# The last feed-forward product in two pieces: 388 tokens with features on the partitions, 128 tokens with tokens on the partitions

## The chip, the cores and the metric

The kernel runs on one core of one Trainium2 chip. The metric is the device time of one execution in microseconds; lower is better. The engines are named as in the profile: PE (TensorE), DVE (VectorE), ACT (ScalarE), POOL (GpSimd) and SP (SyncE, which only issues DMAs here).

## What is computed

One layer of a hybrid decoder for 1024 prompt positions and 8 sample rows, 1032 tokens of 1024 features. What matters here is the end of the layer: the feed-forward part and the second layer norm, over the features of each token.

```python
x1 = layer_norm(DN_ALPHA * x + mix, ln1_g, ln1_b)
ff = jnp.square(jax.nn.relu(x1 @ w_up + b_up)) @ w_down + b_down
ple = jax.nn.sigmoid(x1 @ w_ple_gate + b_ple_gate) * (p @ w_ple)
x2 = layer_norm(DN_ALPHA * x1 + ff + ple, ln2_g, ln2_b)
```

The output `o_y` has features on its rows (8 blocks of 128 features by 1032 tokens) and is put in order after the launch.

## The kernel before

Activations lie with features on the partitions: `acc[m]`, m = 0 to 7, is a block of 128 features by 1032 tokens, and holds the sum that the second layer norm takes. HF = 516 is half of the tokens, QT = 258 a quarter. Every f32 operand of a product is split into two parts of a shorter type, high and low (`split`, line 107: ACT copies the high part, DVE subtracts for the low one), and a product is three matmuls: high by high, high by low, low by high (`kmm`, line 1517).

The down projection is done by Strassen's scheme in seven products, in the order `DNO` (line 1425): P1, P2, P6, P7, P4, P5, P3. Each works on half of the tokens, half of the k range (16 slices of 128) and four blocks of 128 output features, `mp` = 0 to 3. The weights of a product are eight tiles of 128 by 1024: `dn_raw` (line 1450) loads a tile with one DMA on SP into one of three `raw` buffers, `split` turns it into high and low. For P3 the source is `sd["S4"]`, sums of weights that the kernel wrote to DRAM earlier. Four of the eight tiles of P3 go into the four rotating `hl` buffers, the last four (`n` = 52 to 55) into tiles named `dh`. Tile `2 * mp + c` holds the k slices 8c to 8c + 7 of block `mp`. The activations of a product are `hop[96 + k]`, k = 0 to 15, in SBUF.

The last product, P3, only adds to the second half of the tokens, blocks `acc[0]` to `acc[3]`. It is written out at the end of the kernel (the loops over `q` and `mp`): for each of the two quarters q = 2, 3 and each `mp`, 48 matmuls of 258 columns into a PSUM tile of `region2` (three in rotation), then a DVE add into `acc[mp]`. `sum_` keeps a running sum of the blocks in `sum2`.

The layer norm of feature-major tokens needs sums over partitions. They are f32 matmuls with a 128 by 128 matrix of equal values, `ones`, which leave the mean on every partition. `rsqrt_` (line 804) is an inverse root in nine dependent DVE operations. Quarter 2 is normalised by the generator `ln_steps` (line 1057), pulled while quarter 3 is multiplied. Quarter 3 is normalised by `ln_last` (line 1598) in steps: the mean of the first five finished blocks is subtracted early, squares are gathered as blocks finish, steps 7 and 8 put partial sums onto TensorE at k = 9 and 13 of the last block; step 9 does the rest: the last square, two reductions, the inverse root, and for each block a product with gain and inverse root on DVE, a scale and shift on ACT, and an output DMA (`ln2_out`, line 1514, on SP or ACT's queue). Its centering of six blocks is done by TensorE with `ident` and `nident` into PSUM.

The framework orders the instructions of each engine itself by readiness and program order; so operations of two parts that don't depend on each other mix on an engine. A value normaliser with tokens on the partitions exists elsewhere in the kernel (`v_norm`, line 840: `bn_stats`, `bn_aggr`, the same `rsqrt_` on a column for each token); so does a load in four DMAs with 512-byte pieces (`A_v`, line 184, for `w_v`).

## Time and profile before

| what | value |
|---|---|
| time, median of 3 runs | 1369.5 us (1369.17 to 1370.01) |
| time of the profiled execution | 1369.48 us |
| its span | 1367.7 us |
| TensorE busy | 1357.4 us, 99% |
| DVE busy | 907.6 us, 66% |
| ACT busy | 499.5 us, 37% |
| HBM over the span | 167 GB/s |

The span runs from the first to the last event of the core; the rest of the time lies around it. A busy time counts stretches in which an engine has at least one instruction in work. Matmuls are pipelined, so a matmul's duration is longer than the distance to the next one; the distance (pitch) is what counts for a sum. An f32 matmul stands as two records.

### The profile page before, as it was taken

To read this page: it belongs to the slowest core of one execution; us is meant where nothing else is said; L and a number is where in the kernel's file an instruction comes from. 1 tells how busy PE (TensorE), PEld (TensorE's weight loads), DVE (VectorE), ACT (ScalarE), POOL (GpSimd) and SP (SyncE) were. 2 spreads that over 40 slices of the span, in tenths; PEclk is the share of its full clock that TensorE was granted. 3 is DMA by queue.
4 is the path that set the end of the run, shared out by engine and by line. 5 is a ranking of instruction groups with operands and counts; after the bars stand their busy time and mean duration, and the time that the engine had idled before them with its cause. 6 is when DMAs were issued, how large, how long until landed. Compare 5 with 4: busy or idle time off the path is not lost.

```text
span 1367.7 us, 24910 instructions
## 1 busy us (share of the span) xinstructions
PE 1357.4 (99%) x10222; PEld 1336.6 (98%) x10222; DVE 907.6 (66%) x1590; ACT 499.5 (37%) x694; POOL 195.5 (14%) x318
## 2 busy tenths in 40 slices
PE   9999999999999999999999999999999999999997
PEld 8999999988999999999999999999999999999997
DVE  8929348346476656996787767755665575466957
ACT  3231231222241133554234444444454433244423
POOL 0320310125021112000003333201100000000000
PEclk9999999999999999999999999999999999999999
DMA  7573564532256667342346677645478764565421
GB/s 262 147 181 101 148 156 111 154 114 70 71 197 236 231 224 249 107 133 93 109 133 229 231 271 248 219 149 171 135 234 275 278 225 165 179 213 196 137 94 62
DMA packets 104418, 237.20 MB, mean 173 GB/s; under 512 B 11736, under 2 KB 40552, under 8 KB 104304
## 3 DMA queue, kind: packets, MB, share of 16 engines
q1 hardware_dynamic: 76800, 159.84, 37.1%
q0 software_dynamic: 22128, 72.09, 15.1%
q10 hardware_dynamic: 5376, 3.68, 1.1%
q8 instruction: 80, 1.31, 0.4%
q14 instruction: 34, 0.28, 0.1%
HBM read 160.72 MB, written 68.16 MB: 167 GB/s over the span
## 4 chain that ended last, share of the span: by engine, by line
PE 97%; DVE 1%; DMA 0%; issue 0%; ACT 0%; SPq 0%; ACTq 0%; DVEq 0%
PE q L1174 38%; PE q L1541 19%; PE big L146 8%; PE big L123 6%; PE big L124 6%; PE big L125 6%; PE q L1521 1%; PE q L1520 1%; PE q L1522 1%; PE vps L877 1%; PE vps L876 1%; PE vps L875 1%; PE sps L597 1%; PE kps L543 1%; PE gps L921 1%; PE yps L702 1%
## 5 line engine op out<-in xcount | busy, mean ns | idle before, releaser
L86 DVE TENSOR_TENSOR hl<-raw,hl 128x1024 fp32r<-128x1024 f32 (+1 forms) x174 | 210.3, 1210 | 158.3 <-ACT hl L109 157.1
L1541 PE MATMUL q<-hop,hl 128*128 128x258 f32 x2304 | 277.8, 283 | 0.0
L1541 PEld LDWEIGHTS q<-hop,hl 128*128 128x128 f32 x2304 | 277.3, 190 | 0.1
L109 ACT ACTIVATE hl<-raw 128x1024 fp32r<-128x1024 f32 x171 | 180.6, 1056 | 249.0 <-PE q L1541 113.0
L1174 PE MATMUL q<-xb,hl 128*128 128x258 f32 x1920 | 238.2, 283 | 0.0
L1174 PEld LDWEIGHTS q<-xb,hl 128*128 128x128 f32 x1920 | 234.0, 190 | 0.1
L1174 PE MATMUL q<-xT,hl 128*128 128x258 f32 x1536 | 189.7, 283 | 0.0
L1174 PEld LDWEIGHTS q<-xT,hl 128*128 128x128 f32 x1536 | 186.7, 190 | 0.0
L123 PE MATMUL big<-xh,hl 128*128 128x344 f32 x504 | 163.1, 324 | 0.0
L125 PE MATMUL big<-xh,hl 128*128 128x344 f32 x504 | 161.4, 320 | 0.0
L124 PE MATMUL big<-xl,hl 128*128 128x344 f32 x504 | 161.2, 320 | 0.0
L123 PEld LDWEIGHTS big<-xh,hl 128*128 128x128 f32 x504 | 94.7, 188 | 0.7 <-issue 0.2
L124 PEld LDWEIGHTS big<-xl,hl 128*128 128x128 f32 x504 | 94.7, 188 | 0.4 <-issue 0.4
L125 PEld LDWEIGHTS big<-xh,hl 128*128 128x128 f32 x504 | 94.7, 188 | 0.0
L1174 PE MATMUL q<-mgh,hl 128*128 128x258 f32 x480 | 78.6, 285 | 0.0
L86 DVE TENSOR_TENSOR hop<-hraw,hop 128x516 fp32r<-128x516 f32 x112 | 71.6, 691 | 8.7 <-ACT hop L1498 8.3
L1174 PEld LDWEIGHTS q<-mgh,hl 128*128 128x128 f32 x480 | 66.8, 190 | 0.1
L1498 ACT ACTIVATE hop<-hraw 128x516 fp32r<-128x516 f32 x90 | 53.6, 629 | 29.5 <-DMA hraw<-hd 21.7
L959 POOL DMA_DIRECT2D dsum<-w_down x48 | 25.8, 541 | 242.8 <-DVE raw L86 75.3
L739 ACT ACTIVATE sg<-big,vec 128x1032 f32<-128x1032 f32 x16 | 18.0, 1126 | 94.9 <-issue 55.7
L1174 PE MATMUL q<-mgl,hl 128*128 128x258 f32 x240 | 48.2, 282 | 0.0
L83 DVE SCALAR_TENSOR_TENSOR hA<-q,vec,pu 128x516 f32<-128x516 f32 x32 | 24.1, 753 | 27.8 <-issue 14.6
(392 smaller groups left out, 2045.6 us busy)
## 6 DMA issues: line engine op xcount, KB each, us to landing
hraw<-hd SPq DMA_DIRECT2D x52, 516.0 KB, 5.4
dsum<-w_down POOLq DMA_DIRECT2D x48, 256.0 KB, 4.4
gd<-sg SPq DMA_DIRECT2D x16, 516.0 KB, 4.1
hd<-tA POOLq DMA_DIRECT2D x16, 516.0 KB, 3.5
hd<-hB POOLq DMA_DIRECT2D x16, 516.0 KB, 6.2
hd<-tB POOLq DMA_DIRECT2D x16, 516.0 KB, 6.9
raw<-w_gate SPq DMA_DIRECT2D x16, 512.0 KB, 4.3
raw<-w_out SPq DMA_DIRECT2D x16, 512.0 KB, 4.4
```

The source lines that it names most:

```text
L83: eng.scalar_tensor_tensor(out=out, in0=in0, scalar=sc, in1=in1, op0=op0, op1=op1)
L86: eng.tensor_tensor(out=out, in0=a, in1=b, op=op)
L109: S.activation(out=hi, in_=src, func=AF.Copy)
L123: T.matmul(out, wh, xh[:, sl], start=(start and k == 0), stop=False)
L124: T.matmul(out, wh, xl[:, sl], start=False, stop=False)
L125: T.matmul(out, wl, xh[:, sl], start=False, stop=(stop and k == last))
L146: T.matmul(ps[:, t, 0:TT], w_, x_[:, t * TT:(t + 1) * TT], start=st_, stop=sp_)
L739: S.activation(out=f3(sg), in_=fv(ps), func=AF.Sigmoid, bias=col("b_ga" if m < 8 else "b_gb", m % 8))
L959: eng.dma_start(out=r_[:, 512 * k:512 * k + 512], in_=i["w_down"][(2 * n + g) * 4 + m // 2][:, (m % 2) * 512:(m % 2) * 512 + 512])
L1174: T.matmul(ps[j][:, 0:QT] if isinstance(ps, list) else ps[:, j, 0:QT], w_, x_[:, j * QT:(j + 1) * QT], start=st_, stop=sp_, skip_group_che ...
L1498: S.activation(out=u[:, 0, :], in_=src, func=AF.Copy)
L1541: T.matmul(ps[:, j, 0:QT], w_, x_[:, quarter(j)], start=st_, stop=sp_, skip_group_check=True)
```

## The change

`dn_raw` loads the tiles of P3 in another arrangement, with four DMAs for a tile: tile j holds the k slices 2j and 2j + 1 of all four blocks. The second half of the tokens is cut into 388 (`slA`) and 128 (`slC`). For the 388 tokens the product stays feature-major: blocks 0 and 1 together with k outermost, then 2 and 3, with matmuls of 388 columns. Their layer norm, `lnA`, has the steps of `ln_last`, without the centering by TensorE; steps 9 to 16 are the output of one block each. For the 128 tokens the product is made with tokens on the partitions: the activations are the stationary operand, and the weights of all four blocks move, 512 columns. `flip` adds the sums so far in `acc` to it: a matmul with `ident` turns a block of `acc` into token rows, blocks 4 to 7 into the PSUM bank Y, blocks 0 to 3 onto the product in the bank X. Then the rows are normalised: `bn_stats` of Y and X, `bn_aggr`, `rsqrt_` on one column, scaling into `zt`, eight matmuls with `ident` that turn the rows back, gain and shift on ACT and DVE by turns, and four output DMAs of two blocks each, by SP and POOL in turn. The last two blocks of the 388 tokens come after that in the text. Quarter 2's own `ln_steps` goes.

```diff
@@ -1451,6 +1451,14 @@
         r_ = raw_()
         if pr in ("P1", "P2", "P4"):
             dn_load(r_, mp + DNW[pr][0], DNW[pr][1], kh)
+        elif pr == "P3":
+            j = 2 * mp + kh
+            dst = r_.rearrange("p (k m c) -> p m k c", k=2, m=4)
+            for m in range(4):
+                c = (2 * j % 8) * 128
+                nc.sync.dma_start(out=dst[:, m], in_=sd["S4"][2 * m + j // 4][:, c:c + 256].rearrange(
+                    "p (k c) -> p k c", k=2))
         else:
             nc.sync.dma_start(out=r_, in_=sd[DNW[pr]][2 * mp + kh])
         return r_
@@ -1592,24 +1600,25 @@
             tt(V, sum2[:, sl], acc[ms[0]][:, sl] if first and k == 1 else sum2[:, sl],
                acc[m][:, sl], ALU.add)
 
+    NA = HF - 128
+    slA, slC = slice(HF, HF + NA), slice(HF + NA, NTOK)
-    def ln_last(t0, n, step_):
...
+    def lnA(step_):
+        xs_ = [acc[m][:, slA] for m in perm]
+        a, b, x, d2, dl, ssq, q4, q5, q6 = (tmpA[k] for k in (
+            "a", "b", "x", "d2", "dl", "ssq", "q4", "q5", "q6"))
+        y = sum2[:, slA]
...
+                elif m == 4:
+                    tt(V, ssq, ssq, q4, ALU.add)
+                elif m > 4:
+                    tt(V, ssq, ssq, sq, ALU.add)
+            if step_ == 6:
+                tt(V, y, xs_[5], xs_[6], ALU.add)
...
             pm, pv = (pss.tile([128, 512], F32, tag="sm", name=nm) for nm in ("mps", "vps"))
+            tmpA["p"] = (pm[:, 0:NA], pv[:, 0:NA])
+            T.matmul(pm[:, 0:NA], ones, y, start=True, stop=False, skip_group_check=True)
+            T.matmul(pv[:, 0:NA], ones, ssq, start=True, stop=False, skip_group_check=True)
+        pm, pv = tmpA["p"]
         if step_ == 8:
+            S.activation(out=b, in_=xs_[7], func=AF.Square)
+            T.matmul(pm, ones, xs_[7], start=False, stop=True, skip_group_check=True)
+            T.matmul(pv, ones, b, start=False, stop=True, skip_group_check=True)
+            S.activation(out=d2, in_=pm, func=AF.Square)
+            S.activation(out=dl, in_=pm, func=AF.Copy)
+            stt(V, x, pv, EPS, d2, ALU.add, ALU.subtract)
+            rsqrt_(y, x, a, b)
             return
...
-            if m not in cen:
...
-        for m in range(4, 8):
-            center(m, ident, xs_[m], True)
-        for m in range(2, 8):
-            center(m, nident, dl, False)
-        for m in range(2):
-            tt(V, xs_[m], xs_[m], dl, ALU.subtract)
-            cen[m] = xs_[m]
-        rsqrt_(y, x, a, b)
-        for m in range(8):
-            stt(V, xs_[m], cen[m], col("ln2_g", perm[m]), y, ALU.mult, ALU.mult)
-            if m in (7,):
-                ts(V, xs_[m], xs_[m], RS_K, col("ln2_b", perm[m]), ALU.mult, ALU.add)
-            else:
-                S.activation(out=xs_[m], in_=xs_[m], func=AF.Identity, scale=RS_K,
-                             bias=col("ln2_b", perm[m]))
-            ln2_out(perm[m], sl)
+        m = step_ - 9
+        tt(V, xs_[m], xs_[m], dl, ALU.subtract)
+        stt(V, xs_[m], xs_[m], col("ln2_g", perm[m]), y, ALU.mult, ALU.mult)
+        S.activation(out=xs_[m], in_=xs_[m], func=AF.Identity, scale=RS_K, bias=col("ln2_b", perm[m]))
+        ln2_out(perm[m], slA)
...
-    otags = otags[-8:]
-    assert len(otags) == 8
+    assert len(otags) == 10
+    (ztag, ytag), otags = otags[0:2], otags[2:]
+    ds = {k: bpool.tile([128, HF], F32, tag=f"ds{k}", name=f"lnd{k}") for k in (0, 2, 3)}
+    for k, (u, c) in {"a": (tmp2, 0), "b": (tmp2, HF), "x": (tmpv, 0), "d2": (tmpv, HF),
+                      "dl": (tmpw, 0), "ssq": (tmpw, HF), "q4": (ds[0], 0), "q5": (ds[2], 0),
+                      "q6": (ds[3], 0)}.items():
+        tmpA[k] = u[:, c:c + NA]
...
-    nident = bpool.tile([128, HF], F32, tag="ds2", name="nident")[:, 0:128]
-    ts1(V, nident, ident, -1.0, ALU.mult)
-    for q in range(2, 4):
-        sl = quarter(q)
-        sum_([4, 5, 6, 7], sl, True)
-        for mp in range(4):
-            r_ = region2()[:, 0, 0:QT]
+    def wcol(k, m=None):
+        w = wdn[48 + k // 2]
+        c0 = (k % 2) * 512
+        c = slice(c0, c0 + 512) if m is None else slice(c0 + m * 128, c0 + m * 128 + 128)
+        return w[0][:, c], w[1][:, c]
+    def hsl(k, lo, hi):
+        return tuple(z_[:, lo:hi] for z_ in hop[96 + k])
+    sum_([4, 5, 6, 7], slA, True)
+    r2 = region2()
+    for k in range(16):
+        for mp in range(2):
+            kmm(r2[:, mp, 0:NA], wcol(k, mp), hsl(k, 0, NA), k == 0, k == 15)
+    tt(V, acc[0][:, slA], acc[0][:, slA], r2[:, 0, 0:NA], ALU.add)
+    tt(V, sum2[:, slA], sum2[:, slA], acc[0][:, slA], ALU.add)
+    lnA(4)
+    for mp in range(1, 4):
+        if mp > 1:
+            r2 = region2()
             for k in range(16):
-                w = wdn[48 + 2 * mp + k // 8]
-                c = slice((k % 8) * 128, (k % 8) * 128 + 128)
-                x_ = hop[96 + k]
-                kmm(r_, (w[0][:, c], w[1][:, c]),
-                    (x_[0][:, quarter(q - 2)], x_[1][:, quarter(q - 2)]), k == 0, k == 15)
-                if q == 3 and mp == 3 and k in (9, 13):
-                    ln_last(q * QT, QT, 7 if k == 9 else 8)
...
+                kmm(r2[:, 0, 0:NA], wcol(k, mp), hsl(k, 0, NA), k == 0, k == 15)
+                if mp == 3 and k == 11:
+                    lnA(7)
+        else:
+            for m in range(1, 4):
+                tt(V, acc[m][:, slA], acc[m][:, slA], dl, ALU.subtract)
+        tt(V, acc[mp][:, slA], acc[mp][:, slA], r2[:, 1 if mp == 1 else 0, 0:NA], ALU.add)
+        if mp < 3:
+            lnA(4 + mp)
+    XY = region2()
+    X, Y = XY[:, 0, :], XY[:, 1, :]
...
+    zt = unit(ztag, F32, [128, 1024], name="zt")
+    def flip(dst, m):
+        T.matmul(dst[:, (m % 4) * 128:(m % 4) * 128 + 128], acc[m][:, slC], ident,
+                 start=m > 3, stop=m > 3, skip_group_check=True)
+    for k in range(16):
+        (wh, wl), (ah, al) = wcol(k), hsl(k, NA, HF)
+        T.matmul(X, ah, wh, start=k == 0, stop=False, skip_group_check=True)
+        T.matmul(X, ah, wl, start=False, stop=False, skip_group_check=True)
+        T.matmul(X, al, wh, start=False, stop=k == 15, skip_group_check=True)
+        if k == 1:
+            lnA(8)
+        if 2 <= k < 6:
+            flip(Y, k + 2)
+        elif 6 <= k < 10:
+            flip(X, k - 6)
+        if k == 6:
+            V.bn_stats(out=st6[:, 1, :], in_=Y)
+    for m in range(6):
+        lnA(9 + m)
+    V.bn_stats(out=st6[:, 0, :], in_=X)
+    V.bn_aggr(out=mv, in_=st6)
+    x, y, a, b = tin
+    ts1(V, x, mv[:, 1:2], EPS, ALU.add)
+    rsqrt_(y, x, a, b)
+    ts1(V, y, y, RS_K, ALU.mult)
+    stt(V, x, mv[:, 0:1], -1.0, y, ALU.mult, ALU.mult)
+    for h in range(4):
+        src = XY[:, h // 2, 256 * (h % 2):256 * (h % 2) + 256]
+        dst = zt[:, 256 * h:256 * h + 256]
+        if h % 2:
+            S.activation(out=dst, in_=src, func=AF.Identity, scale=y, bias=x)
+        else:
+            ts(V, dst, src, mv[:, 0:1], y, ALU.subtract, ALU.mult)
+    O_ = region2()
+    ot = unit(ytag, F32, [128, 8, 128], name="ot")
+    for m in range(8):
+        ps = O_[:, m // 4, 128 * (m % 4):128 * (m % 4) + 128]
+        T.matmul(ps, zt[:, 128 * m:128 * m + 128], ident, start=True, stop=True, skip_group_check=True)
+        if m % 2:
+            S.activation(out=ot[:, m], in_=ps, func=AF.Identity, scale=col("ln2_g", m), bias=col("ln2_b", m))
+            (nc.sync if m % 4 == 1 else nc.gpsimd).dma_start(
+                out=o["o_y"][m - 1:m + 1, :, slC].rearrange("m p n -> p m n"), in_=ot[:, m - 1:m + 1])
+        else:
+            ts(V, ot[:, m], ps, col("ln2_g", m), col("ln2_b", m), ALU.mult, ALU.add)
+    for m in range(6, 8):
+        lnA(9 + m)
```

## Rows read from the trace of the kernel before

**Rows 1.** The page: busy times and instructions by engine; chain by engine.

```profile
PE 1357.4 (99%) x10222; PEld 1336.6 (98%) x10222; DVE 907.6 (66%) x1590; ACT 499.5 (37%) x694; POOL 195.5 (14%) x318
...
PE 97%; DVE 1%; DMA 0%; issue 0%; ACT 0%; SPq 0%; ACTq 0%; DVEq 0%
```

**Rows 2.** Busy times by stretch: each engine, granted clock, DMA share, GB/s.

```profile
1303.60:1353.50 49.90, 49.90 (x403) 49.40 (x402) 30.50 (x70) 14.84 (x29) 0.00 (x0) 1.00 0.23 75
...
1353.50:1363.90 10.40, 6.10 (x29) 4.96 (x27) 8.61 (x22) 4.16 (x10) 0.00 (x0) 0.98 0.15 50
```

**Rows 3.** Timeline of PE at the last product: start, us, operation.

```profile
1303.41 0.28 PE L1520 MATMUL q<-hop,hl 128*128 128x258 f32 x1
...
1353.23 0.28 PE L1522 MATMUL q<-hop,dh 128*128 128x258 f32 x1
...
1356.83 2.77 PE L1642 MATMUL q<-lnt,nident 128*128 128x258 f32 x12
```

**Rows 4.** Timeline of PE at f32 matmuls of 128 columns.

```profile
336.20 1.95 PE L921 MATMUL gps<-wst,vt 128*128 128x128 f32 x16
...
337.90 0.40 PE L123 MATMUL big<-xh,hl 128*128 128x344 f32 x1
```

**Rows 5.** Timeline of PE at matmuls of 344 and 512 columns.

```profile
321.72 0.32 PE L124 MATMUL big<-xl,hl 128*128 128x344 f32 x1
...
324.39 0.32 PE L123 MATMUL big<-xh,hl 128*128 128x344 f32 x1
...
283.35 0.39 PE L877 MATMUL big<-hl,xl 128*128 128x512 f32 x1
...
287.53 0.39 PE L877 MATMUL big<-hl,xl 128*128 128x512 f32 x1
```

**Rows 6.** Timeline of SP, ACT and DVE: late weight tiles of the last product.

```profile
1304.20 6.51 SPq L1455 DMA_DIRECT2D raw<-S4d  x4
...
1308.05 1.06 ACT L109 ACTIVATE dh<-raw 128x1024 fp32r<-128x1024 f32 x1 [3.30 <-DMA raw<-S4d]
...
1309.14 1.23 DVE L86 TENSOR_TENSOR dh<-raw,dh 128x1024 fp32r<-128x1024 f32 x1 [0.48 <-ACT dh L109]
...
1315.70 1.23 DVE L86 TENSOR_TENSOR dh<-raw,dh 128x1024 fp32r<-128x1024 f32 x1 [1.21 <-ACT dh L109]
```

**Rows 7.** Timeline of SP, and landing times, of the `w_v` loads.

```profile
226.74 2.53 SPq L189 DMA_DIRECT2D raw<-w_v  x4
...
DMA to landing us min/median/max: 2.3/2.9/4.1
```

**Rows 8.** Timeline of DVE after the last product: first and last operation.

```profile
1353.55 0.42 DVE L86 TENSOR_TENSOR acb<-acb,q 128x258 f32<-128x258 f32 x1 [3.16 <-PE q L1522]
...
1363.56 0.36 DVE L89 TENSOR_SCALAR acb<-acb,vec 128x258 f32<-128x258 f32 x1
```

**Rows 9.** Timeline of DVE at 516 and 258 columns.

```profile
1269.24 2.51 DVE L86 TENSOR_TENSOR acb<-acb,lnx 128x516 f32<-128x516 f32 x4
...
1361.08 2.45 DVE L83 SCALAR_TENSOR_TENSOR acb<-q,vec,sum 128x258 f32<-128x258 f32 x6
```

**Rows 10.** Timeline of DVE in the value path's normaliser.

```profile
289.35 0.69 DVE L884 BATCH_NORM_STATS2 vst<-vt 128x6 f32<-128x512 f32 x1 [0.70 <-ACT vt L883]
...
290.30 0.17 DVE L92 TENSOR_SCALAR nwt<-vmv 128x3 f32<-128x3 f32 x1
...
292.49 2.44 DVE L89 TENSOR_SCALAR vt<-vt,vmv,nwt 128x512 f32<-128x512 f32 x3
```

**Rows 11.** DMA issues: queue, count, KB each, median us to landing.

```profile
o_y<-acb SPq DMA_DIRECT2D x12, 129.0 KB, 2.0
...
yd<-Y POOLq DMA_DIRECT2D x16, 64.0 KB, 3.2
...
o_state<-outst POOLq DMA_DIRECT2D x1, 16.0 KB, 1.7
```

**Rows 12.** Busy times in the 0.1 us in which the granted clock fell.

```profile
1363.40:1363.50 0.10, 0.00 (x0) 0.00 (x0) 0.10 (x1) 0.10 (x2) 0.00 (x0) 0.57 0.27 73
```

More of the change, by code (lines that the diff above doesn't have):

```diff
@@ L1593, in sum_ @@
                acc[m][:, sl], ALU.add)
+    NA = HF - 128
+    slA, slC = slice(HF, HF + NA), slice(HF + NA, NTOK)
     perm = [4, 5, 6, 7, 0, 1, 2, 3]
-    lastp = []
-    def ln_last(t0, n, step_):
-        sl = slice(t0, t0 + n)
-        xs_ = [acc[m][:, sl] for m in perm]
-        a, b, x = (tmp2[:, k * TT:k * TT + n] for k in range(3))
-        d2, dl = (tmpv[:, k * TT:k * TT + n] for k in range(2))
-        y, ssq = sum2[:, sl], tmpv[:, 2 * TT:2 * TT + n]
-        q4, q5, q6 = (tmpw[:, k * TT:k * TT + n] for k in range(3))
+    tmpA = {}
+    def lnA(step_):
[3 more added lines that the diff above has]
+        y = sum2[:, slA]
         if step_ < 7:
@@ L1610, in ln_last @@
                 pm = pss.tile([128, 512], F32, tag="sm", name="mps")
-                T.matmul(pm[:, 0:n], ones5, y, start=True, stop=True)
-                V.tensor_copy(out=dl, in_=pm[:, 0:n])
+                T.matmul(pm[:, 0:NA], ones5, y, start=True, stop=True)
+                V.tensor_copy(out=dl, in_=pm[:, 0:NA])
             for m in (range(5) if step_ == 4 else (step_,)):
@@ L1624, in ln_last @@
             pm, pv = (pss.tile([128, 512], F32, tag="sm", name=nm) for nm in ("mps", "vps"))
-            lastp.extend((pm, pv))
-            T.matmul(pm[:, 0:n], ones, xs_[5], start=True, stop=False, skip_group_check=True)
-            T.matmul(pv[:, 0:n], ones, ssq, start=True, stop=False, skip_group_check=True)
+            tmpA["p"] = (pm[:, 0:NA], pv[:, 0:NA])
+            T.matmul(pm[:, 0:NA], ones, y, start=True, stop=False, skip_group_check=True)
+            T.matmul(pv[:, 0:NA], ones, ssq, start=True, stop=False, skip_group_check=True)
@@ L1628, in ln_last @@
             return
-        pm, pv = lastp
+        pm, pv = tmpA["p"]
         if step_ == 8:
-            T.matmul(pm[:, 0:n], ones, xs_[6], start=False, stop=False, skip_group_check=True)
-            for sq in (q4, q6):
-                T.matmul(pv[:, 0:n], ones, sq, start=False, stop=False, skip_group_check=True)
-            return
-        cen = {}
-        def center(m, e, v, st_):
-            if m not in cen:
-                r_ = region2()
-                for j in range(2):
-                    cen[m + j] = r_[:, j, 0:n]
-            T.matmul(cen[m], e, v, start=st_, stop=not st_, skip_group_check=True)
@@ L1644, in ln_last @@
-        S.activation(out=b, in_=xs_[7], func=AF.Square)
-        center(2, ident, xs_[2], True)
-        T.matmul(pm[:, 0:n], ones, xs_[7], start=False, stop=True, skip_group_check=True)
-        center(3, ident, xs_[3], True)
-        T.matmul(pv[:, 0:n], ones, b, start=False, stop=True, skip_group_check=True)
-        S.activation(out=d2, in_=pm[:, 0:n], func=AF.Square)
-        S.activation(out=dl, in_=pm[:, 0:n], func=AF.Copy)
-        stt(V, x, pv[:, 0:n], EPS, d2, ALU.add, ALU.subtract)
-        for m in range(4, 8):
-            center(m, ident, xs_[m], True)
@@ new lines, in hybrid_step_kernel @@
+    XY = region2()
+    X, Y = XY[:, 0, :], XY[:, 1, :]
+    st6 = bpool.tile([128, 2, 6], F32, tag="st6", name="st6")
+    mv = bpool.tile([128, 2], F32, tag="mv", name="mv")
+    tin = [bpool.tile([128, 3], F32, tag=f"nwt{k}", name="nwl")[:, 0:1] for k in range(4)]
+    zt = unit(ztag, F32, [128, 1024], name="zt")
[15 more added lines that the diff above has]
+            V.bn_stats(out=st6[:, 1, :], in_=Y)
```

19 lines of the change are left out of this document (1 added, 18 removed).

## The prediction

> **What bounds the kernel now.** I read the page first: TensorE is busy for 99% of the span, and the chain that ended last is 97% TensorE, so an edit counts where it shortens TensorE's queue or the stretch behind it [rows 1]. Next come the busy times of the last stretches [rows 2]: from 1303.6 to 1353.5 us TensorE has no idle time, and in the 10.4 us after that DVE is busy for 8.61 while TensorE only finishes small products. DVE's last operation ends at 1363.92 [rows 8]; in the 3.78 us from there to 1367.7 nothing computes and the outputs land. So two things can be won: the 49.9 us of the last product, and the 14.2 us behind it. The profiled execution took 1369.48 us for a span of 1367.7, 1.78 more, and the median of the runs is 1369.5, so a difference of the span can be put on the median as it stands.
>
> **The product on TensorE.** It starts at 1303.41 and its last matmul starts at 1353.23 [rows 3]; with a pitch of 0.12 it holds the queue until 1353.35, for 49.94 us. In it are 384 matmuls of 258 columns and nine f32 reductions of 258 columns. One f32 matmul shows as two records; eight of 128 columns took 337.90 - 336.20 = 1.70 [rows 4], 0.2125 each, so one of 258 columns 0.43 and the nine 3.87. That leaves 46.07 / 384 = 0.120 each. The change has 192 matmuls of 388 columns and 48 of 512. The pitch at 344 columns is (324.39 - 321.72) / 17 = 0.157, at 512 columns (287.53 - 283.35) / 18 = 0.232 [rows 5]; between them 388 columns come to 0.177. So 192 x 0.1767 = 33.93 and 48 x 0.2322 = 11.15: 45.08, a gain of 1.0, from fewer instructions. Five f32 reductions stay, 388 columns wide: 0.43 x 388/258 = 0.647, in all 3.23. Eight turns of `acc` into token rows (`flip`) are f32 matmuls of 128 columns: 1.70. Sum: 50.01 us, against 49.94. The product itself gains nothing; its end moves from 1353.35 to 1353.42. The `ident` and `nident` matmuls of the old centering go; they lay beside DVE's chain, so that is worth nothing.
>
> **The weights of the product.** Before, each pair of tiles served one block of features, and the last four were needed only from the third block on. Now every tile holds two k of all four blocks, and all eight are read within the first two blocks: 12 matmuls a tile, 2.12 us. With tiles numbered from 0, tile j is needed at 1303.41 + 2.12 j: tile 4 at 1311.9, tile 7 at 1318.3. Their supply in the trace: SP issues the four late loads from 1304.20 on, ACT starts on tile 4 at 1308.05, DVE ends it at 1309.14 + 1.23 = 1310.4, and tile 7 at 1315.70 + 1.23 = 1316.9 [rows 6]. The slack is 1.5 and 1.35 us, where it was 4.5 and 6.7 (tile 4 was first read after 96 matmuls of 0.12, tile 7 after 168). Each load also becomes four DMAs of 128 KB in 512-byte pieces on SP, 32 issues in place of 8. The loads of `w_v` have the same form [rows 7]: a burst of four took 2.53 us of SP, and a part landed after 2.9 (2.3 to 4.1). The last part is issued some 1.9 after the first, so a tile is there after 4.8, against 3.85 for the single DMA of tile 4 (1304.20 to 1308.05). I take 0.8 later, as parts overlap. The load of tile 7 waits for the buffer of tile 4, so the delay e counts twice: stall = 2e - 1.35 = 0.25, I take 0.3. The ends: e = 0, no stall; issue 2.1 and landing 4.1, so e = 2.3 and a stall of 3.3. Behind SP's loads stand only outputs of the first half, for which nobody waits then.
>
> A rule speaks against the split. The rows above show a part of 128 KB landing after 2.9, the whole of 512 KB after 3.85. The Trainium skill, "DMA: Bandwidth & Descriptors", section "Measured", lists 0.95 us for 64 KB and 6.15 us for 1 MB and advises large DMAs. An estimate by those two figures is 1.3 us for 128 KB and 3.4 for 512 KB; four parts in turn would cost e = 1.8 and a stall of 2.25, and the sum below would be 1369.0.
>
> **Behind the product.** Before: the add of the last block starts 0.32 after its last matmul (1353.23 to 1353.55), and DVE ends at 1363.56 + 0.36 [rows 8], 10.57 after the queue's end: squares, two reductions, a chain of nine dependent operations for the inverse root, eight products.
>
> The 388 tokens. The same chain now lies beside the row product, which takes 11.15 + 1.70 + 1.29 = 14.1 us on TensorE. An operation of 516 columns on DVE has a pitch of 0.61 (2.51 for four), one of 258 out of PSUM 0.41 (2.45 for six) [rows 9], so 388 columns come to 0.51. From the end of the feature-major part (1339.6 with the stall): add, square, two reductions, 2.9 us, so the scalar chain starts at 1342.5. Then 0.5 + 4.1 (root; two of its nine steps are shorter) + 3.1 (six subtractions) + 0.7 (row statistics of the first half) + 3.1 (six products) = 11.5 us, to 1354.0 when gaps are filled, and 1355.0 when the last two subtractions come first too. The row product is readable at 1353.72 + 0.2 = 1353.92. So DVE is the later one by 0.1 to 1.1; I take 0.35, nearer the lower end, as most operands lie in SBUF: the row statistics start at 1354.27. The cover is thin: each operation of 388 columns that doesn't fit costs its 0.5 us.
>
> The 128 tokens. The value path has the same steps [rows 10]: statistics of 512 columns and aggregate 0.95 (289.35 to 290.30), eleven small operations 2.19 (290.30 to 292.49); here one more, 0.20: 3.34. I add 0.2 for operations of the 388 tokens that slip into the chain's gaps (0 to 2.0: four of them). Scaling the first 256 columns out of PSUM: 0.45, from the 0.41 and a semaphore. The first turn back can start at 1354.27 + 3.34 + 0.2 + 0.45 = 1358.26. Eight take 1.70 [rows 4], with ACT or DVE emptying each beside the next; 0.2 and 0.3 for the last: 1360.46, 3.46 us earlier than 1363.92.
>
> The outputs. Before, 3.78 us lie between DVE's end and the span's end, of which 2.0 are the landing [rows 11]. Now the last pair goes by POOL, whose landings run from 1.7 (16 KB) to 3.2 (64 KB) [rows 11]; 128 KB of short rows by POOL has no row. I take 2.6: 3.78 + 0.6 = 4.4, so 1364.85. The last two features of the 388 tokens need DVE between the emptyings until about 1360.9, then ACT 0.55, and SP: 1361.45 + 3.78 = 1365.2, which is later and sets the end. The change is 1365.2 - 1367.7 = -2.5: **1367.0 us**.
>
> **The rivals.** (1) The clock falls before the turns back. TensorE idles from 1353.7 to 1358.3, 4.5 us. In the trace the granted clock left 1.00 for 0.50 (2.4 and 1.2 GHz) in the 0.1 us from 1363.4, whose mean is 0.57 [rows 12], 3.8 us after the last matmul ended (1356.83 + 2.77) [rows 3]; one fall doesn't show how constant these 3.8 are. At 1.2 GHz eight turns take twice 1.70: POOL's path ends at 1366.5, time 1368.3. The Trainium skill, "TensorE: Matmul & The Clock Gate", section "HAM oscillation", states this as a rule: a wait between groups of matmuls makes the next group start cold. By it the time is 1368.3. Chance 0.22.
> (2) The product starves at tiles 4 to 7. It ends above 1369.5 once the stall exceeds 2.8, that is a tile over 2.1 us later than now. At the end of the rows, e = 2.3: 1370.0, and with the low clock too 1371.3. For it: slack 1.35, a delay that counts twice. Against: the median part of `w_v`. Chance 0.13 from 1368.5 on, 0.07 of it above 1372.2.
> (3) The change doesn't overlap what it should: DVE finishes all eight features of the 388 tokens ahead of the row statistics' chain. Four operations, +2.0 less the 0.2 counted; the wait for TensorE grows to over 6 us, so the turns are slow, +1.7. POOL then sets the end: 1364.85 + 3.5 = 1368.35, time 1370.1. Chance 0.10.
> (4) Each doubtful term at its lower end (no stall, no lag, no slip, the last two features early, POOL as for 16 KB): -1.4, 1365.6. Chance 0.13.
>
> **How the numbers follow.** The forecast, 1366.3 to 1367.9, has 0.42. A measurement here tells about 0.2% from no change: below 1366.8 or above 1372.2. Faster: (4) and half of the forecast's band, 0.34. Slower: 0.07 from (2) and 0.03 from (3) with a stall. Same: 0.56. The range goes from 1365.4, rival (4), to 1371.3, starving at the end of its rows with the low clock.
>
> **What would show it.** Right: 50 us from the first to the last matmul of the product; no idle TensorE in its first two blocks; row statistics within 1 us of the last row matmul; turns back at 0.21 us each; last computation at 1360.5 to 1361.5. Wrong: TensorE waiting for `dh` tiles; a clock of 0.50 at the turns (0.42 us each); subtractions or products of `acb` between the one-column operations; a POOL landing over 3.2.

## The result, and the profile after

The kernel after the change takes 1376.6 us (median; 1376.17 to 1377.37), the kernel before 1369.4 beside it: ratio 1.0052, 95% interval 1.0040 to 1.0065, so 7 us slower. The forecast was 1367.0, and the upper end of the range 1371.3. The profiled execution has a span of 1374.5 us, 6.8 more than before.

The page after the change, its busy times and its chain by engine, beside [rows 1]:

```profile
PE 1358.3 (99%) x10074; PEld 1333.0 (97%) x10074; DVE 907.0 (66%) x1575; ACT 498.6 (36%) x685; POOL 196.5 (14%) x320
...
PE 80%; issue 19%; DMA 1%; DVE 0%; SPq 0%; POOL 0%; ACT 0%; POOLq 0%
```

The busy times are almost those of before. The page can't show where 7 us went: the chain now ends at POOL's last output, and its long "issue" is only POOL's pause before that. One has to go to the end of the span. Busy times by stretch (length; PE, weight load, DVE, ACT, POOL; granted clock; DMA share; GB/s), beside [rows 2, 12]:

```profile
1303.35:1354.85 51.50, 50.42 (x268) 46.60 (x266) 32.93 (x58) 13.39 (x22) 0.00 (x0) 1.00 0.21 62
...
1357.10:1357.20 0.10, 0.00 (x0) 0.00 (x0) 0.07 (x2) 0.02 (x1) 0.00 (x0) 0.74 0.82 295
1357.20:1359.40 2.20, 0.00 (x0) 0.00 (x0) 1.87 (x10) 0.00 (x0) 0.00 (x0) 0.50 0.26 96
1359.40:1370.20 10.80, 6.37 (x16) 4.01 (x16) 2.09 (x5) 2.96 (x6) 0.73 (x1) 0.50 0.12 36
1370.20:1374.50 4.30, 0.00 (x0) 0.00 (x0) 0.00 (x0) 0.00 (x0) 0.73 (x1) 0.50 0.10 30
```

Two things stand out. In the product TensorE has 1.08 us without work, where before it had none. And from 1359.40 to 1370.20, the stretch of the eight turns back, no engine is busy for even 60% of the time: PE 6.37, DVE 2.09, ACT 2.96 of 10.80. 6.37 + 2.09 + 2.96 = 11.4 is close to the whole stretch, as it would be if the engines worked one after the other. The timeline shows that they do. TensorE first (start, duration, operation, idle time before it and what ended it; beside [rows 3]):

```profile
1303.35 0.34 PE L1528 MATMUL q<-hop,hl 128*128 128x388 f32 x1
...
1347.98 0.50 PE L1741 MATMUL q<-hl,hop 128*128 128x512 f32 x1 [1.08 <-DVE st L1751]
...
1354.81 0.40 PE L1743 MATMUL q<-dh,hop 128*128 128x512 f32 x1
1359.40 0.79 PE L1772 MATMUL q<-ident,zt 128*128 128x128 f32 x2 [4.19 <-DVE zt L89]
1360.96 0.80 PE L1772 MATMUL q<-ident,zt 128*128 128x128 f32 x2 [0.76 <-DVE ot L89]
1362.30 0.80 PE L1772 MATMUL q<-ident,zt 128*128 128x128 f32 x2 [0.55 <-ACT ot L1774]
1363.61 0.80 PE L1772 MATMUL q<-ident,zt 128*128 128x128 f32 x2 [0.51 <-DVE ot L89]
...
1368.90 0.80 PE L1772 MATMUL q<-ident,zt 128*128 128x128 f32 x2 [0.50 <-DVE ot L89]
```

Then DVE, ACT and POOL in the same stretch (beside [rows 8, 10]):

```profile
1347.24 0.69 DVE L1751 BATCH_NORM_STATS2 st<-q 128x6 f32<-128x512 f32 x1
...
1355.25 0.70 DVE L1754 BATCH_NORM_STATS2 st<-q 128x6 f32<-128x512 f32 x1 [0.16 <-PE q L1743]
1355.86 0.61 DVE L83 SCALAR_TENSOR_TENSOR acb<-acb,vec,sum 128x388 f32<-128x388 f32 x1
...
1358.81 0.54 DVE L89 TENSOR_SCALAR zt<-q,mv,nwl 128x256 f32<-128x256 f32 x1
1360.04 0.54 DVE L89 TENSOR_SCALAR zt<-q,mv,nwl 128x256 f32<-128x256 f32 x1 [0.69 <-ACT zt L1765]
1360.50 0.40 DVE L89 TENSOR_SCALAR ot<-q,vec 128x128 f32<-128x128 f32 x1
1363.14 0.41 DVE L89 TENSOR_SCALAR ot<-q,vec 128x128 f32<-128x128 f32 x1 [2.24 <-PE q L1772]
...
1359.44 0.56 ACT L1765 ACTIVATE zt<-q,nwl 128x256 f32<-128x256 f32 x1 [2.32 <-DVE zt L89]
...
1361.80 0.46 ACT L1774 ACTIVATE ot<-q,vec 128x128 f32<-128x128 f32 x1 [0.61 <-PE q L1772]
...
1369.73 0.46 ACT L1774 ACTIVATE ot<-q,vec 128x128 f32<-128x128 f32 x1 [2.19 <-PE q L1772]
...
1370.48 0.73 POOL L1775 DMA_DIRECT2D o_y<-ot  x1 [4.56 <-ACT ot L1774]
```

Follow one step: the turn at 1360.96 ends at 1361.76; ACT empties it from 1361.80 to 1362.26; the next turn starts at 1362.30, though its input was scaled by 1360.00 (1359.44 + 0.56) and its columns of PSUM were free. A step is 0.80 + 0.04 + 0.46 + 0.04 = 1.34 with ACT and 1.31 with DVE, and there are eight in line (the first takes 1.56, as DVE scales a piece of `zt` before it empties): from the first turn to the last emptying (1369.73 + 0.46 = 1370.19) 10.79 us, where the forecast had 2.2.

The weights, which the prediction feared, are harmless. Timeline of SP, ACT and DVE and the landing of the parts, beside [rows 6]:

```profile
1304.06 8.78 SPq L1460 DMA_DIRECT2D raw<-S4d  x16
...
1308.61 1.06 ACT L109 ACTIVATE dh<-raw 128x1024 fp32r<-128x1024 f32 x1 [3.99 <-DMA raw<-S4d]
...
1316.62 1.23 DVE L86 TENSOR_TENSOR dh<-raw,dh 128x1024 fp32r<-128x1024 f32 x1 [1.32 <-ACT dh L109]
...
raw<-S4d SPq DMA_DIRECT2D x16, 128.0 KB, 3.1
```

Tile 4 comes 0.56 later than before (1308.61 against 1308.05), tile 7 0.92 later (1316.62 against 1315.70), and TensorE has no wait in the first two blocks.

### The profile page after: what moved, and what is told of

It reads as the page before. It is cut to its first block, busy times and chain, and to the rows that moved or that the text cites. A ratio compares the mean times of both kernels' runs of the same rounds, so it can differ in the third digit from the quotient of the medians.

```text
span 1374.5 us, 24623 instructions
## 1 busy us (share of the span) xinstructions
PE 1358.3 (99%) x10074; PEld 1333.0 (97%) x10074; DVE 907.0 (66%) x1575; ACT 498.6 (36%) x685; POOL 196.5 (14%) x320
## 3 DMA queue, kind: packets, MB, share of 16 engines
q8 instruction: 79, 1.29, 0.4%
## 4 chain that ended last, share of the span: by engine, by line
PE 80%; issue 19%; DMA 1%; DVE 0%; SPq 0%; POOL 0%; ACT 0%; POOLq 0%
PE q L1174 38%; PE big L146 8%; PE q L1549 6%; PE big L123 6%; PE big L124 6%; PE big L125 6%; PE vps L877 1%; PE vps L876 1%; PE vps L875 1%; PE sps L597 1%; PE kps L543 1%; PE gps L921 1%; PE yps L703 1%; PE yps L702 1%; PE big L322 1%
```

## The experiments

The theory after this reading: users of one PSUM tile are put in line, so a turn into the tile `O_` waits until the emptying of the turn before it has read, although it writes other columns, or another bank. Rivals: the low clock alone (each turn takes 0.41 instead of 0.21); the SBUF tiles `zt`, which holds the scaled rows, and `ot`, into which the emptyings write; the chip's PSUM banks in place of the program's tiles. Every kernel below is the kernel after the change with the named edit, or, where the text says so, another of these kernels with it; `...` marks what is left out of an edit. The ratio is to the kernel before, run beside it (1369.5 to 1369.8).

**The turns in four PSUM tiles.** Both turns of a pair stand ahead of their two emptyings.

```diff
-    O_ = region2()
+    Os = [region2()[:, 0], region2()[:, 0], pss.tile([128, 512], F32, tag="sm", name="o2"),
+          pss.tile([128, 512], F32, tag="sm", name="o3")]
...
     for m in range(8):
-        ps = O_[:, m // 4, 128 * (m % 4):128 * (m % 4) + 128]
-        T.matmul(ps, zt[:, 128 * m:128 * m + 128], ident, start=True, stop=True, skip_group_check=True)
+        ps = Os[m // 2][:, 128 * (m % 2):128 * (m % 2) + 128]
+        if m % 2 == 0:
+            for j in range(2):
+                T.matmul(Os[m // 2][:, 128 * j:128 * j + 128], zt[:, 128 * (m + j):128 * (m + j) + 128],
+                         ident, start=True, stop=True, skip_group_check=True)
```

> Edit: the eight turns back go two by two into four PSUM tiles, both turns of a pair ahead of their two emptyings, where all eight shared one tile. Theory (shared tile): in the changed kernel a turn waits until the emptying before it has read its part of the same PSUM tile, so turns and emptyings alternate at 1.32 us; apart, only the turns' own 0.41 (low clock) and the pieces of zt bound them, the last emptying ends near 1363.7 in place of 1370.2, and the time falls by about 6.5 to 1370. Rival (clock alone): the turns are slow because the clock is at 0.50; then this edit changes less than 1 us. Rival (shared SBUF tile ot holds up the emptyings): DVE and ACT still alternate at 0.46 each, last emptying near 1364.5, the emptyings never overlap.

Measured: 1370.5 us, ratio 1.0006 [0.9996, 1.0015]: 6.2 us back of the 7. Its timeline, TensorE, the first emptying and the last:

```profile
1359.92 2.01 PE L1775 MATMUL q<-ident,zt 128*128 128x128 f32 x8 [4.19 <-DVE zt L89]
1361.72 1.88 PE L1775 MATMUL o<-ident,zt 128*128 128x128 f32 x8
...
1361.12 0.41 DVE L89 TENSOR_SCALAR ot<-q,vec 128x128 f32<-128x128 f32 x1
...
1364.09 0.46 ACT L1778 ACTIVATE ot<-o,vec 128x128 f32<-128x128 f32 x1 [0.36 <-DVE ot L89]
```

The turns are almost back to back, and first turn to last emptying is 4.63 us instead of 10.79: 6.2 less, the whole gain. The rest of the kernel is the same. So the line of turns and emptyings is the cause of the slowdown. The low clock alone is not: it was low here too, from 1360.1 to 1363.4. The last emptying came at 1364.55, which is what the rival of the shared `ot` expected (1364.5), and DVE and ACT still empty almost by turns; the run with one reader for each tile, below, tells whether `ot` does that.

**Two loops in place of one.** The same single tile, but all eight turns stand ahead of all eight emptyings.

```diff
     for m in range(8):
         ps = O_[:, m // 4, 128 * (m % 4):128 * (m % 4) + 128]
         T.matmul(ps, zt[:, 128 * m:128 * m + 128], ident, start=True, stop=True, skip_group_check=True)
+    for m in range(8):
+        ps = O_[:, m // 4, 128 * (m % 4):128 * (m % 4) + 128]
         if m % 2:
```

> The changed kernel with its last loop cut in two: all eight turns stand first in the program, then all eight emptyings. The one PSUM tile and all else stay. It asks what a shared tile makes wait. If only a turn that stands behind an emptying in the program waits for it (each emptying of the same tile holding back the next turn, 1.32 us a step), the eight turns now follow each other at 0.41 us, and the emptyings follow by turns of DVE and ACT at the 0.43 us a step seen with the turns in pairs: last emptying about 1364.0 instead of 1370.19, time 1370.3 us. If an emptying also waits until all eight turns into its tile are done, they start 2.9 us later: 1372.8. If neither holds and a turn simply takes 1.3 us, it stays at 1376.6.

Measured: 1373.0 us, ratio 1.0024 [1.0015, 1.0034], at the second theory's 1372.8. TensorE, then DVE and ACT:

```profile
1361.11 3.40 PE L1772 MATMUL q<-ident,zt 128*128 128x128 f32 x16 [4.19 <-DVE zt L89]
...
1364.55 0.41 DVE L89 TENSOR_SCALAR ot<-q,vec 128x128 f32<-128x128 f32 x1 [2.26 <-PE q L1772]
1365.48 0.41 DVE L89 TENSOR_SCALAR ot<-q,vec 128x128 f32<-128x128 f32 x1 [0.53 <-ACT ot L1776]
...
1364.99 0.46 ACT L1776 ACTIVATE ot<-q,vec 128x128 f32<-128x128 f32 x1 [2.10 <-DVE ot L89]
```

The turns now follow each other, but the first emptying starts at 1364.55, when the last turn has ended (1361.11 + 3.40), though its own, 0.80 long, was done some 2.6 us earlier; and DVE and ACT then read the tile strictly in turns, 0.47 us each. So all users of the tile stand in line, readers among themselves too, in the order of the text. (In this profile the product begins and ends 1.7 us later than in the kernel after the change, hence the later times.)

**The banks in turn.** The turns in the order 0, 4, 1, 5, ..., so that each goes to the other bank of the tile than the one before; DVE empties one bank, ACT the other.

```diff
-    for m in range(8):
+    for m in (0, 4, 1, 5, 2, 6, 3, 7):
...
+        if m > 3:
+            S.activation(out=ot[:, m], in_=ps, func=AF.Identity, scale=col("ln2_g", m), bias=col("ln2_b", m))
+        else:
+            ts(V, ot[:, m], ps, col("ln2_g", m), col("ln2_b", m), ALU.mult, ALU.add)
...
```

> The changed kernel with its eight turns in the order 0, 4, 1, 5, 2, 6, 3, 7, so that they go to the two PSUM banks of the shared tile in turn; DVE empties one bank, ACT the other. Two outputs of pairs come at the end instead of being spread. If a turn waits only for readers of its own bank, two chains of four steps run beside each other and 4 x 1.32 = 5.3 us go: 1371.3 us. If it waits for the reader of the tile whichever bank that reads, the eight steps stay in line at 1.32 us, and only the closeness of the last two outputs is added: 1376.6 to 1377.2 us.

Measured: 1377.2 us, ratio 1.0056 [1.0039, 1.0072]: nothing gained. Its second and third turn:

```profile
1360.75 0.80 PE L1772 MATMUL q<-ident,zt 128*128 128x128 f32 x2 [0.76 <-DVE ot L89]
1362.10 0.80 PE L1772 MATMUL q<-ident,zt 128*128 128x128 f32 x2 [0.55 <-ACT ot L1774]
```

The turn at 1360.75 writes the second bank and waits for DVE's reading of the first. The line goes by the tile, not by the bank. The waits are in the program itself: the list of TensorE's instructions of the kernel after the change, as built, gives each turn a wait on the engine that emptied the one before (the first of the two in the first line waits for `zt`). The fifth turn, the first into the second bank, waits for the emptying of the fourth like the others.

```
4304 L1772 MATMUL q<-ident,zt 128x128 [waits DVE_49] x2
4305 L1772 MATMUL q<-ident,zt 128x128 [waits Activation_49]
4306 L1772 MATMUL q<-ident,zt 128x128 [waits DVE_49]
```

The Trainium skill, "PSUM — Partial Sum Buffer", section "PSUM bank collisions raise a hardware error", says that two engines may not use one bank on the same partitions at the same time, two readers included, and that software must put such uses in line. The trace agrees as far as it goes: no turn here overlaps a reading of its bank, and in the order of the change, four turns into each bank, that rule alone would already put every turn but the first into each bank behind the emptying before it. The run with the banks in turn shows more than the rule asks: there the waits cross banks.

**X and Y in two PSUM tiles.** This asks for the price of the same thing in the row product.

```diff
-    XY = region2()
-    X, Y = XY[:, 0, :], XY[:, 1, :]
+    X, Y = region2()[:, 0, :], region2()[:, 0, :]
...
```

> Edit: the row product's banks X and Y become two PSUM tiles. Theory (shared tile): the row product no longer waits 1.1 us for the statistics of Y, and DVE's piece of Y no longer waits for ACT's piece of X if that was the shared PSUM tile; the time falls by 1.1 to 1.3 us, to about 1375.4. Rival (the wait is for DVE being late with other work, not for the tile): no change.

Measured: 1376.5 us, ratio 1.0047 [1.0032, 1.0062]. The expected 1375.4 did not come, and the number is that of the rival, "no change"; the trace shows that the wait went all the same. Its DVE and ACT:

```profile
1354.38 0.69 DVE L1753 BATCH_NORM_STATS2 st<-q 128x6 f32<-128x512 f32 x1
...
1358.30 0.99 DVE L89 TENSOR_SCALAR zt<-q,mv,nwl 128x256 f32<-128x256 f32 x2
...
1358.93 1.02 ACT L1764 ACTIVATE zt<-q,nwl 128x256 f32<-128x256 f32 x2 [2.08 <-DVE zt L89]
```

The 1.08 us in which X's matmul waited for the statistics of Y are gone, and those of X start 0.87 earlier. The pieces of `zt` are scaled by two engines beside each other. But two products of `acb` instead of one now slip in behind the statistics (at 1354.99 and 1355.63, 0.61 and 0.57 us): DVE has them to do before the end anyway, and the earlier chain only lets them in. The first turn starts 0.5 earlier (1358.89), and little of that arrives.

**`zt` in two SBUF tiles.**

```diff
-    zt = unit(ztag, F32, [128, 1024], name="zt")
+    zts = [unit(ztag, F32, [128, 1024], name="zt"), raw_()]
...
```

> Edit: zt becomes two SBUF tiles, one written by DVE and one by ACT. If the shared SBUF tile makes the four scalings run one after the other (0.54 and 0.56 us in turn), they now run two at a time; if reading the same PSUM tile does it, nothing changes. In both cases the turns behind stay the bound, so the time stays within 0.5 us of the changed kernel's 1376.6.

Measured: 1377.0 us, ratio 1.0051 [1.0035, 1.0067], no gain; the four scalings stay in line (1358.64, 1359.28, 1359.87, 1360.45). With X and Y apart and one `zt` they ran beside each other. It was the shared PSUM tile of X and Y that held them, not `zt`.

**The clock alone.** 18 f32 matmuls of 128 columns, result unused, written behind the row product.

```diff
     V.bn_stats(out=st6[:, 0, :], in_=X)
+    dm = pss.tile([128, 512], F32, tag="sm", name="dm")
+    for _ in range(18):
+        T.matmul(dm[:, 0:128], ones, ones, start=True, stop=True, skip_group_check=True)
```

> Edit: 18 f32 matmuls of 128 columns into an unused PSUM tile behind the row product, so that TensorE has work while the rows are normalised; the eight turns stay in one tile. Theory (shared tile): the clock stays at 1.00 up to the turns, each step of turn and emptying falls from 1.32 to about 0.95, 8 x 0.35 = 2.8 us less, near 1373.8. Rival (clock alone): the turns take 0.21 each without further waits, the whole stretch shrinks from 10.8 to about 2.5 us and the time to about 1368.5.

Measured: 1375.6 us, ratio 1.0041 [1.0026, 1.0056], where the theory expected 1373.8. TensorE:

```profile
1346.63 1.50 PE L1757 MATMUL dm<-ones 128*128 128x128 f32 x12
...
1354.92 2.84 PE L1757 MATMUL dm<-ones 128*128 128x128 f32 x24
1359.18 0.49 PE L1775 MATMUL q<-ident,zt 128*128 128x128 f32 x2 [1.42 <-DVE zt L89]
1360.17 0.80 PE L1775 MATMUL q<-ident,zt 128*128 128x128 f32 x2 [0.50 <-DVE ot L89]
```

Six of the 18 ran inside the product, where X's matmul waits for the statistics of Y, and twelve behind it. The first turn ran at the full clock (0.49 instead of 0.80, and a step of 0.99), the clock fell after 1360.0, and the other seven turns took 0.80. So this run did not keep the clock for the turns, and cannot rule the clock out by itself; its one step at full clock still waits for the emptying, 0.99 where the clock alone would leave 0.21. What rules the clock out as the whole cause is the run with the turns apart.

**The clock once the turns are apart.** The kernel with the turns in four tiles, with the edit of the run before this one (18 matmuls into `dm`).

> The kernel with the turns in pairs in four PSUM tiles (1370.5), and 18 f32 matmuls of 128 columns behind the row product into an unused PSUM tile (extra work, result unused); X and Y still share a tile, and each tile of the turns is still emptied by two engines. Clock theory: eight turns at 0.21 us in place of 0.41 give 1.7 us, 1368.8. Theory that the emptyings, one after the other at 0.43 us, set the pace whatever the clock: only the first pair is earlier, 0.4 us, 1370.0.

Measured: 1369.6 us, ratio 0.9999 [0.9990, 1.0008]: 0.9 better than without, between the two theories and nearer to the emptyings' pace. Here too twelve of the 18 lay behind the product (2.84 us), but the clock stayed at 1.00 through all eight turns. First turn to last emptying is 3.92 us (1358.94 to 1362.86) instead of 4.63.

**One reader for each tile.** X and Y apart, the turns in four tiles, and each tile read by one engine only.

```diff
+    X, Y = region2()[:, 0, :], region2()[:, 0, :]
...
-        if h % 2:
+        if h > 1:
...
+    for p in (0, 2, 1, 3):
+        ps = (region2()[:, 0] if p in (0, 2) else pss.tile([128, 512], F32, tag="sm", name=f"o{p}"))[:, 0:256]
...
+            if p > 1:
```

> X and Y in two PSUM tiles, and the turns in pairs in four PSUM tiles, each tile read by one engine: X scaled by DVE and Y by ACT, features 0 to 3 emptied by DVE and 4 to 7 by ACT, in the order of pairs 0, 2, 1, 3. The work is the same. If sharing a PSUM tile is what serialised the product, the scalings and the emptyings, then against the kernel with only the turns in pairs (1370.5) it gains 1.1 us at the row product, about 1.1 at the four scalings (two beside two) and little at the emptyings while the turns run at the low clock (0.41 us each), less 0.6 for a further product of acb that slips in, as with X and Y apart: 1368.9 us (1368.4 to 1369.5). If only the turns mattered, it stays at 1370.5.

Measured: 1369.9 us, ratio 1.0000 [0.9991, 1.0010], 0.5 better than with the turns apart alone, where 1.6 was expected. The scalings are beside each other, but first turn to last emptying is 4.63 us again (1359.35 to 1363.98): sixteen records of turns at 0.50 of the clock take 3.77 by themselves, and nothing beside them counts.

**One reader for each tile, and the clock.** The 18 matmuls of above in the kernel with one reader, and the last pair's output on SP.

```diff
-        (nc.sync if p % 2 == 0 else nc.gpsimd).dma_start(
+        (nc.sync if p in (0, 3) else nc.gpsimd).dma_start(
```

> The kernel with one reader for each PSUM tile, and besides 18 f32 matmuls of 128 columns into an unused PSUM tile behind the row product (extra work, result unused), and the last pair's output on SP, pair 1's on POOL. 18 take 3.8 us at full clock, from about 1354.3 to 1358.1, so the clock should still be 1.00 when the first turn starts near 1358.9. If the low clock then costs what eight turns at 0.41 instead of 0.21 us add, 1.7 us, and SP saves 0.4: 1367.2 us (1366.7 to 1367.8). If the emptyings set the pace by now, only about 0.5: 1368.4.

Measured: 1368.4 us, ratio 0.9991 [0.9981, 1.0000]; 1.5 better than without. TensorE's end:

```profile
1353.66 4.18 PE L1756 MATMUL dm<-ones 128*128 128x128 f32 x36
1358.93 1.37 PE L1775 MATMUL q<-ident,zt 128*128 128x128 f32 x8 [1.09 <-DVE zt L89]
1360.14 1.06 PE L1775 MATMUL o<-ident,zt 128*128 128x128 f32 x8
```

Eight turns take 2.27 us instead of 3.77, and first turn to last emptying 3.11 (1358.93 to 1362.04). All of the 1.5 us lies there: from the last emptying to the span's end it is 4.5 us (to 1366.5), against 4.3 without, so the output on SP gave nothing. The expectation's 1368.4, for emptyings that set the pace, is met by chance: it was counted from 1368.9 for the kernel without, which took 1369.9. The clock's price, 1.5 us, appears in full only when nothing else holds the turns back: 0.9 with two readers for a tile. DVE and ACT at the emptyings:

```profile
1360.79 0.73 DVE L89 TENSOR_SCALAR ot<-o,vec 128x128 f32<-128x128 f32 x2 [0.38 <-PE o L1775]
...
1360.34 0.81 ACT L1781 ACTIVATE ot<-q,vec 128x128 f32<-128x128 f32 x2 [0.80 <-PE q L1775]
```

Both write `ot` from 1360.79 to 1361.15, so the shared `ot` holds nobody up; what put the emptyings in line was the PSUM tile.

**The products of `acb` out of the row chain.** In the kernel of the run before, the products of the last two features get a gain column that depends on the chain's end.

```diff
+        g_ = gl[m - 6] if m > 5 else col("ln2_g", perm[m])
...
+    gl = [a, b]
+    for m in range(6, 8):
+        stt(V, gl[m - 6], x, 0.0, col("ln2_g", perm[m]), ALU.mult, ALU.add)
```

> The kernel with one reader for each PSUM tile and the clock kept (1368.4), and the products with gain and root of the last two features of the 388 tokens made to depend on the end of the row chain (their gain column is written again from the chain's last value, two one-column operations more). In the trace of the kernel without this they stood between the row statistics of X and the one-column operations, 0.6 and 0.5 us. If DVE's order sets the end, the chain ends 1.1 us earlier, and the two products lie between the emptyings, where DVE waits 0.4 us twice for TensorE: 1367.5 us (1367.2 to 1368.2). If the last two features then land last, as the prediction assumed for the changed kernel, the gain is given back: 1368.4.

Measured: 1368.6 us, ratio 0.9992 [0.9983, 1.0001]: no gain on 1368.4, the case in which the last two features land last. The last operations of DVE and ACT are now theirs:

```profile
1360.79 0.61 DVE L83 SCALAR_TENSOR_TENSOR acb<-acb,nwl,sum 128x388 f32<-128x388 f32 x1
...
1361.52 0.62 ACT L1656 ACTIVATE acb<-acb,vec 128x388 f32<-128x388 f32 x1
```

The first turn starts 0.71 earlier (1358.22), but SP issues its last output until 1362.57, little before the 1362.90 at which POOL was done without this edit. DVE is busy for 10.20 of the 10.90 us from 1350.5 to 1361.4, so its work is close to being the limit, and its order only decides what comes last; this is read from the trace, no run tests it alone.

**Three products on POOL.** The kernel is again that with one reader and the clock kept; three of its four last outputs go by SP.

```diff
+        if m in (5, 6, 7):
+            tt(nc.gpsimd, xs_[m], xs_[m], y, ALU.mult)
+            S.activation(out=xs_[m], in_=xs_[m], func=AF.Identity, scale=gk[:, perm[m]:perm[m] + 1],
+                         bias=col("ln2_b", perm[m]))
```

> The kernel with one reader for each PSUM tile and the clock kept (1368.4), the products of the last three features of the 388 tokens with the root moved to POOL (one tensor by tensor product each; the gain goes into the scale of ACT's step, from one added operation of 8 columns at the start), and of the four last outputs three on SP instead of two. On the value path POOL took 6.46 us for four operations of this kind with 512 columns, so 1.2 us for 388; three from 1351.2 end near 1354.9, beside DVE. DVE has three operations of 0.48 to 0.55 us less, one ahead of the row statistics (which then start when the product ends, 1354.0) and two behind them: chain 1.5 us earlier, SP 0.4: 1366.5 us (1366.2 to 1367.2). Rival: POOL and DVE slow each other where both work, DVE's operations of 388 columns grow: 1368 or more.

Measured: 1369.0 us, ratio 0.9995 [0.9986, 1.0003]: the rival's case. DVE and POOL where both work:

```profile
1351.70 5.16 DVE L83 SCALAR_TENSOR_TENSOR acb<-acb,vec,sum 128x388 f32<-128x388 f32 x5
...
1351.75 3.63 POOL L86 TENSOR_TENSOR acb<-acb,sum 128x388 f32<-128x388 f32 x3 [227.35 <-DVE sum L83]
```

POOL's three take 1.21 each as worked out, but DVE's five take 5.16, where six take 3.29 in the kernel without: 1.03 each instead of 0.55. That is a mean of two paces: the three beside POOL start 1.42, 1.31 and 1.29 before the next one, the last two, after POOL's end at 1355.38, take 0.5 each. The Trainium skill, "GPSIMD Engine Reference", section "1. Specifications", says that this engine shares its SBUF interfaces with VectorE and contends with its instructions of two SBUF inputs; the trace agrees, with 1.3 to 1.4 beside POOL against 0.55 without it.

**One product moved, three outputs on SP.** In the kernel with one reader and the clock kept, only the last feature's product depends on the chain's end.

```diff
+    stt(V, gl, x, 0.0, col("ln2_g", perm[7]), ALU.mult, ALU.add)
...
-        (nc.sync if p in (0, 3) else nc.gpsimd).dma_start(
+        (nc.gpsimd if p == 2 else nc.sync).dma_start(
```

> The kernel with one reader for each PSUM tile and the clock kept (1368.4), with only the last feature's product made to depend on the end of the row chain, and three of the four last outputs on SP. In that kernel's trace the last output left on POOL, issued until 1362.90 after the pair's last emptying at 1361.52; on SP it leaves about 0.4 earlier. One product (0.57 us) goes out of the chain and fits where DVE waits for TensorE, with its last step on ACT done before the last emptyings. Expected 1367.7 us (1367.3 to 1368.3), 0.13% below the kernel before. If the end is set by the landing of 512 KB of outputs at once rather than by the time of their issue, 1368.4 as before.

Measured: 1368.2 us, ratio 0.9988 [0.9979, 0.9997], inside the range of what was expected (1367.3 to 1368.3), though not at its 1367.7. It is the lowest median: 8.4 us below the change as it was, and 1.6 below the kernel before. The 0.2 us to the 1368.4 above are less than the intervals tell apart.

## Why the prediction was wrong

**The step that failed** is "Eight take 1.70 [rows 4], with ACT or DVE emptying each beside the next": eight turns and the emptyings behind them as an overlapped 2.2 us. They took 10.79, 8.6 of the 9.7 by which the last emptying came later than forecast (1370.19 against 1360.46). [rows 4] show sixteen records of matmuls back to back; they show no reader between them. The row gave the price of a turn, and the overlap was assumed without a row. No rival held it either: neither the four rivals nor the list of what would make the forecast wrong names a wait between a turn and the emptying before it, and the range ended 5 us too low for that reason.

**The product.** Forecast 50.01 us; with X and Y apart, so without the wait, it ran from 1303.26 to 1353.61 (last matmul at 1353.38, and a pitch of 0.23), 50.35: right to 0.3, of which 0.2 lie in the 388 tokens and 0.1 in the row product. In the kernel after the change it ran from 1303.35 to 1355.04, 51.69: the same cause as above added 1.3 in the middle, with 1.08 of it idle: X's matmul behind the reading of Y's statistics, two halves of one tile. It was not in the sum, and is the second place where the forecast let an engine write and another read one tile at no cost.

**The weights.** Forecast e = 0.8 for the delay of a tile and a stall of 0.3. Measured 0.56 for tile 4 and 0.92 for tile 7, under its slack of 1.35, and no stall. Right in size. The rule weighed there, from the Trainium skill, "DMA: Bandwidth & Descriptors", section "Measured", whose figures are for loads issued from POOL while these go by SP, would have made e 1.8, which the trace does not show. The cover is as thin as it was said to be: in one other profile, that of the turns in four tiles, TensorE waited 0.58 us for a `dh` tile.

**The row statistics.** Forecast: start at 1354.27, with a lag of DVE of 0.35 behind the product. With X and Y apart it was 1354.38, 0.57 behind the readable product (1353.61 + 0.2), with DVE busy until then. In the kernel after the change the late product covers the lag, and they start at 1355.25. The chain from there to the first turn: forecast 3.34 + 0.2 + 0.45 = 3.99, measured 4.15 (1355.25 to 1359.40), with one product of `acb`, 0.61, in place of the 0.2. Right.

**The clock, rival (1).** It fell before the turns, as that rival said, and eight turns without waits took 3.40 us (two loops) instead of 1.70. The 1.7 us it put on this are close to the 1.5 that the runs give where turns set the pace (3.77 against 2.27). In the line of turns and emptyings it costs more, since each turn's latency counts: 1.32 a step against the 0.99 of the one step at full clock, 8 x 0.33 = 2.6 us of the 10.8; this is an estimate from that one step.

**Rivals (2) and (3).** No starving. DVE did finish all eight features early: seven products ahead of the statistics and one just behind, the last step on ACT by 1357.13. That cost nothing, as the product was later by its 1.3 us. With this cover gone two products slip in, 0.61 and 0.57 long. Rival (4)'s terms, added again, give 0.3 + 0.35 + 0.2 for stall, lag and slip, 0.35 from SP's path to POOL's and 0.9 for POOL's landing, so 2.1 and 1364.9 instead of the 1.4 and 1365.6 on record; nothing here turns on it.

**The outputs.** Forecast 4.4 from the last emptying by POOL, measured 1370.19 to 1374.5, 4.3, of which the landing is 2.3 (2.6 forecast). Right. The path by SP that was to set the end lay far ahead.

**Taken together:** 1.0 at the statistics, 0.2 in the chain, 8.6 in turns and emptyings make 9.7. With each cause taken away, the change gives 1368.2 to 1368.6. That this is rival (1)'s 1368.3 is luck: there the clock was low and nothing else, here it was kept, and the time went into products that slip in and into DVE's work. So even with the overlap that the prediction imagined, the change gains 1.0 to 1.6 us, about 0.1%, at the edge of what the intervals tell from none, and needs 18 matmuls of filling for it.

**Open:** a version with the order kept by banks instead of tiles was not tried; it needs another way to order the work. And no run separates DVE's work from the clock and the slips in what is left of the gain.

## What to carry to other kernels

Count PSUM tiles where a sum assumes that a matmul runs beside the reading of an earlier result: in a program that orders work by tiles, columns or banks of one tile are not separate. A chain "matmul, read, matmul, read" into one tile costs the whole latency of both each time, so look for it when a loop writes and empties in one body; give each step in flight a tile of its own and each tile one reader. A price taken from back-to-back rows holds only for work that is back to back; ask of each such term which row shows the overlap.

## What the runs showed of the hardware

The time from the last matmul to the fall of the clock is not constant. In the kernel before it was 3.8 us [rows 3, 12]; after the change 1.9 (1354.81 + 0.40 to the 0.1 us from 1357.10 above, mean 0.74); with X and Y apart 4.8 (1353.78 to the 0.1 us from 1358.6, mean 0.58). In two further runs, with one reader for each tile (last matmul ended 1354.24) and with the turns apart (1355.74), the granted clock by stretch:

```profile
1357.40:1357.50 0.10, 0.00 (x0) 0.00 (x0) 0.08 (x1) 0.00 (x0) 0.00 (x0) 0.94 0.00 0
...
1360.00:1360.10 0.10, 0.10 (x1) 0.10 (x2) 0.00 (x0) 0.10 (x1) 0.00 (x0) 0.59 0.00 0
```

That is 3.2 and 4.3 us. So one pause length does not settle the clock of what follows: 4.19 us without matmuls lie before the first turn both after the change, where it found the clock at 1.2 GHz, and with the turns apart, where it started at 2.4 GHz and the clock fell 0.1 us later. Small matmuls in the pause did not settle it either: with 2.84 us of them behind the product and 1.4 us of pause then, the clock fell 2.3 us after they ended, with one turn between, in the run with the clock alone, and stayed through all eight turns in the run with the turns apart. There the turns came almost back to back, in the first run they waited for their emptyings. With 4.18 us of them and 1.1 us of pause it stayed too.
